# Eight experts on one core: the first two x loads divided by even and odd partitions over two issuing engines

## The chip, the cores and the metric

The kernel runs on 1 core of a Trainium2 chip. The metric is the device time of one execution in microseconds, lower being better; the kernel before has a median of 180.97 us in 3 runs.

## The reference

Eight experts, each with its own 256 tokens, weights and biases, in float32:

```python
# x (8, 256, 512)  w1 (8, 512, 2048)  w2 (8, 2048, 512)  b1 (8, 2048)  b2 (8, 512)
h = np.matmul(x, w1) + b1[:, np.newaxis, :]
h = np.maximum(h, 0)
return (np.matmul(h, w2) + b2[:, np.newaxis, :]).astype(np.float32)
```

## The kernel before

Each expert has two products. The first one, `ph`, is written as 16 groups of 128 hidden columns (`nJ`), each of 4 matmuls over chunks of the 512 inputs (`nKC`). ScalarE reads every group out of PSUM, adds the bias and applies the maximum with zero, which gives `hT` (L231). The second product, `po`, sums 16 of those groups for each of two blocks of 128 tokens. The second product of an expert runs `LAG` = 3 stages behind its first one. A loop of 11 stages on TensorE (`E + LAG`) holds both: matmuls of `ph` are L297, those of `po` L314, the bias b2 as a matmul with ones L324.

Weights come as float32 from HBM and are cast to fp16 by their transfer. All of these transfers are issued by GpSimd at L88 (`load`), 2 MB in SBUF for each of w1 and w2 of an expert, with the loads of x for experts 2 to 7 in two pieces and the stores of experts 0 to 5 behind. They share one queue, q0 in the profile. `NW` = 3 buffers hold w1 and three hold w2. GpSimd waits for a buffer to be free before it issues the load that refills it, so w1 of expert 3 waits for the first product of expert 0. The first weight load waits for the semaphore `s_first`, which a one-row activation on ScalarE (`warm`, L131) raises when it is done.

Ahead of this section, x of experts 0 and 1 is loaded as float32 into `x32[0]` and `x32[1]`, by SyncE, one transfer of 128 partitions with a 4 KB row each (two tokens side by side, `(p tb) h -> p tb h`), in the order expert 0, expert 1. ScalarE issues one transfer for `b1_rows`, 32 rows of 2 KB. Then VectorE casts x of expert 0 to fp16 (L137) and transposes it in 32x32 blocks into `xT` (L124), and ScalarE casts x of expert 1 (L139). All engines but GpSimd enter the section behind these operations, the landing of the x and b1 transfers among them. In the section VectorE turns b1 into `b1T` (L196), which the first activation of `hT` waits for, and then goes on with the transposes of the later experts. SyncE waits for landings and raises a semaphore for TensorE (L246, L247). At the end the stores of experts 6 and 7 leave by SyncE (L251), those two results standing in `x32`.

Of the kernel before, what the change touches and what calls it, by code (L numbers as in the profile page):

```python
# [10 lines left out]
def kernel(  # L11
# [12 lines left out]
    nc = tc.nc  # L24
# [6 lines left out]
    P = 128  # L31
    nTB = T // P
# [15 lines left out]
    def sbuf(name, shape, dtype):  # L48
        return ctx.enter_context(nc.sbuf_tensor(name, shape, dtype))
# [14 lines left out]
    x32 = [sbuf(f"x32_{e}", [P, nTB, H], fp32) for e in range(2)]  # L64
# [42 lines left out]
    def transposes(e):  # L107
# [21 lines left out]

    nc.vector.memset(ones1[:], 1.0)  # L130
    tc.keep_in_program_order(nc.scalar.activation(out=warm[:], in_=ones1[:], func=relu).then_inc(s_first, 1))  # L131
    tc.keep_in_program_order(nc.scalar.dma_start(
        out=b1_rows[:], in_=b1.rearrange("e (b i) -> (e b) i", b=nB)))
    for e in range(2):
        tc.keep_in_program_order(nc.sync.dma_start(
            out=x32[e][:], in_=x[e].rearrange("(p tb) h -> p tb h", tb=nTB)))
    nc.vector.tensor_copy(out=x16[0][0][:], in_=x32[0][:])  # L137
    transposes(0)
    tc.keep_in_program_order(nc.scalar.copy(out=x16[1][0][:], in_=x32[1][:]))  # L139
# [29 lines left out]
    def flush(first):  # L169
        n = GROUPS[first]  # L170
        for tb in range(nTB):
# [7 lines left out]
         in_=b2.rearrange("e h -> (e h)").rearrange("(o f) -> o f", o=1))  # L179
# [15 lines left out]
    for b in range(nB):  # L195
        turned = nc.vector.transpose(  # L196
            out=b1T[b * B : (b + 1) * B, nB - 1 - b : nB - 1 - b + nJ * B],
            in_=b1_rows[:].rearrange("r (i j) -> r j i", j=nJ),
# [23 lines left out]
    for s in range(E + LAG):  # L222
        if s < E:
# [3 lines left out]
            for j in range(nJ):  # L227
# [4 lines left out]
                    out=mine.rearrange("p (tb j k i) -> p j tb k i", tb=nTB, j=nJ, k=split)[:, j],  # L232
                    in_=ph[:, j % NPH, 0:T].rearrange("p (tb i k) -> p tb k i", tb=nTB, k=split),
# [19 lines left out]
    for s in range(E + LAG):  # L253
# [5 lines left out]
        e = s - LAG  # L259
# [112 lines left out]
```

## Time and profile before

| What | Value |
|---|---|
| median of 3 runs | 180.97 us (180.75 to 181.03) |
| profiled execution, its own time | 180.75 us |
| its span in the trace | 179.0 us |
| mean granted TensorE clock | 0.966 |
| busy: PE, DVE, ACT, POOL | 134.6, 86.8, 75.1, 12.7 us |
| HBM read, written | 71.39 MB, 4.19 MB |

The span runs from the first to the last instruction of the program; 1.75 us of the profiled execution's own time lie outside it. DMA shares are of the core's 16 DMA engines together: a share of 1.00 in a stretch of 1 us is 16 us of engine time. Packets are put into the stretch in which they start, so a share in a short stretch can go above 1. q0 is the queue that GpSimd feeds, q1 that of SyncE, q10 that of ScalarE. DMA landings are times from issue until the semaphore of the transfer is complete.

### The profile page before, as it was taken

How to read it: one execution, taken by the hardware profiler on the slowest of the kernel's cores; microseconds unless marked ns; L12 is line 12 of the kernel's file. 1: busy time of each engine (PE TensorE's matmuls, PEld its weight loads, DVE VectorE, ACT ScalarE, POOL GpSimd, SP SyncE). 2: the span in 40 equal slices, each digit the busy share in tenths (PEclk: the TensorE clock that was granted, in tenths of full speed). 3: DMA queues.
4: the chain of work that ended last, by engine and by line, in shares of the span. 5: the costliest groups of instructions: out<-in, count | busy, mean ns of one | idle time of the engine just before them, and what ended most of it. 6: DMA issues, size and time to landing. Idle time of an engine off the chain costs nothing. (4 is left out here: it accounts for less than half of the span.)

```text
span 179.0 us, 3015 instructions
## 1 busy us (share of the span) xinstructions
PE 134.6 (75%) x784; PEld 93.3 (52%) x784; DVE 86.8 (49%) x124; ACT 75.1 (42%) x153; POOL 12.7 (7%) x27
## 2 busy tenths in 40 slices
PE   0004978868699890898988896989698896999960
PEld 0003878858689330785468643884298442434420
DVE  0989938576000299998079916992230003031010
ACT  3201786757677113374087505690387201021010
POOL 4200012020200101001010001000200003010000
PEclk9999999999999999579999999699999999999997
DMA  5989989999999998998999999999899999999996
GB/s 206 277 176 236 234 176 236 231 198 216 236 212 196 236 223 187 234 231 183 231 231 209 205 234 216 194 234 231 179 234 231 194 220 205 222 216 207 330 423 273
DMA packets 3827, 40.46 MB, mean 226 GB/s; under 512 B 449, under 2 KB 465, under 8 KB 1137
## 3 DMA queue, kind: packets, MB, share of 16 engines
q0 software_dynamic: 3200, 38.28, 96.7%
q1 hardware_dynamic: 576, 2.10, 3.0%
q10 hardware_dynamic: 48, 0.07, 0.1%
q14 instruction: 3, 0.02, 0.0%
HBM read 71.39 MB, written 4.19 MB: 422 GB/s over the span
## 5 line engine op out<-in xcount | busy, mean ns | idle before, releaser
L297 PE MATMUL ph<-xT,w_sb 128*128 x512 | 73.2, 307 | 32.5 <-PEq L282 30.1
L297 PEld LDWEIGHTS ph<-xT,w_sb 128*128 x512 | 67.0, 146 | 39.7 <-issue 30.8
L231 ACT ACTIVATE hT<-ph,b1T 128x256 f16<-128x256 f32 x128 | 59.7, 473 | 34.0 <-PE ph L297 30.8
L127 DVE STREAM_TRANSPOSE xT<-x 32x256 f16<-32x256 f16 (+1 forms) x64 | 52.8, 893 | 25.1 <-DMA x<-in_x_dram 21.8
L314 PE MATMUL po<-w_sb,hT 128*128 x256 | 56.6, 379 | 2.2 <-issue 2.2
L314 PEld LDWEIGHTS po<-w_sb,hT 128*128 x256 | 24.9, 97 | 33.0 <-issue 6.9
L211 DVE COPY out<-po 32x512 f32<-32x512 f32 (+1 forms) x20 | 13.8, 688 | 42.8 <-PE po L314 42.6
L211 ACT COPY out<-po 32x512 f32<-32x512 f32 (+1 forms) x20 | 11.5, 577 | 45.9 <-PE po L314 45.7
L88 POOL DMA_DIRECT2D w_sb<-in_w_dram x18 | 9.7, 540 | 137.3 <-PE po L314 70.9
L124 DVE STREAM_TRANSPOSE xT<-x 32x256 f16<-32x256 f16 x32 | 14.0, 436 | 0.5
L211 DVE COPY x<-po 128x512 f32<-128x512 f32 x2 | 1.4, 692 | 13.9 <-PE po L314 13.9
L324 PE MATMUL po<-b_sb,ones 1*128 x16 | 4.8, 378 | 3.7 <-issue 2.3
L211 ACT COPY x<-po 128x512 f32<-128x512 f32 x2 | 1.2, 585 | 14.2 <-PE po L314 14.2
L324 PEld LDWEIGHTS po<-b_sb,ones 1*128 1x128 f16 x16 | 1.5, 91 | 6.5 <-issue 6.2
L196 DVE STREAM_TRANSPOSE b1T<-b_rows 32x512 f32<-32x512 f32 x4 | 4.1, 1025 | 0.5 <-issue 0.5
L139 ACT CAST x<-x 128x1024 f16<-128x1024 f32 x1 | 1.0, 1044 | 3.4 <-DMA x<-in_x_dram 3.4
L137 DVE CAST x<-x 128x1024 f16<-128x1024 f32 x1 | 0.7, 694 | 3.2 <-DMA x<-in_x_dram 3.2
L88 POOL DMA_DIRECT2D out_dram<-out x2 | 1.1, 536 | 9.5 <-DVE out L211 9.5
L131 ACT ACT_TABLE_LOAD x1 | 1.3, 1283 | 0.7 <-PEq L356 0.7
L88 POOL DMA_DIRECT2D x<-in_x_dram x2 | 1.3, 644 | 0.0
L130 DVE MEMSET ones<- 1x128 f16 x1 | 0.2, 165 | 0.9 <-PEq L356 0.9
L88 POOL DMA_DIRECT2D b_sb<-in_b_dram x1 | 0.5, 502 | 0.0
(5 smaller groups left out, 0.7 us busy)
## 6 DMA issues: line engine op xcount, KB each, us to landing
w_sb<-in_w_dram POOLq DMA_DIRECT2D x14, 2048.0 KB, 41.1
w_sb<-in_w_dram POOLq DMA_DIRECT2D x4, 1024.0 KB, 22.3
out_dram<-out POOLq DMA_DIRECT2D x1, 2048.0 KB, 24.7
x<-in_x_dram SPq DMA_DIRECT2D x2, 512.0 KB, 4.0
x<-in_x_dram POOLq DMA_DIRECT2D x1, 1024.0 KB, 34.4
out_dram<-out POOLq DMA_DIRECT2D x1, 1024.0 KB, 17.7
out_dram<-x SPq DMA_DIRECT2D x2, 512.0 KB, 6.8
x<-in_x_dram POOLq DMA_DIRECT2D x1, 512.0 KB, 23.1
```

What stands on the lines that cost most here:

```text
L88: engine.dma_start(**kw).then_inc(landed[key], 16)
L124: last = nc.vector.transpose(out=dst[:, :, g, :, 0, :], in_=block[:, :, :, 0, :])
L127: last = nc.vector.transpose(out=dst[:, tb, g], in_=block[:, tb])
L131: tc.keep_in_program_order(nc.scalar.activation(out=warm[:], in_=ones1[:], func=relu).then_inc(s_first, 1))
L137: nc.vector.tensor_copy(out=x16[0][0][:], in_=x32[0][:])
L139: tc.keep_in_program_order(nc.scalar.copy(out=x16[1][0][:], in_=x32[1][:]))
L196: turned = nc.vector.transpose(out=b1T[b * B : (b + 1) * B, nB - 1 - b : nB - 1 - b + nJ * B], in_=b1_rows[:].rearrange("r (i j) -> r j i" ...
L211: last = copy(out=results[e][at : at + rows, k * nTB + tb, :], in_=po[k * rows : (k + 1) * rows, bank : bank + H])
L231: nc.scalar.activation(out=mine.rearrange("p (tb j k i) -> p j tb k i", tb=nTB, j=nJ, k=split)[:, j], in_=ph[:, j % NPH, 0:T].rearrange("p ...
L297: last = nc.tensor.matmul(ph[:, j % NPH, 0:T], w1_sb[:, bass.ds(w_from + (kc * M + j), P, nJ)], xT[:, bass.ds(x_at + kc * T, T)], start=(k ...
L314: return nc.tensor.matmul(banks[tb], hT[:, bass.ds(h_from + (tb * nJ + j) * P, P)], w2_sb[:, bass.ds(w2_from + j * H, H)], start=False, st ...
L324: nc.tensor.matmul(banks[tb], ones1[:], b2_sb[:, bass.ds(s * H, H)], start=True, stop=False)
```

## The change

Each of the two x loads becomes two transfers of 64 partitions, the even partitions by SyncE and the odd ones by ScalarE, every row still 4 KB. The load of b1 moves from ScalarE to SyncE, behind SyncE's two x halves. The activation that releases the first weight load stands where it stood, ahead of ScalarE's transfers.

```diff
     nc.vector.memset(ones1[:], 1.0)
     tc.keep_in_program_order(nc.scalar.activation(out=warm[:], in_=ones1[:], func=relu).then_inc(s_first, 1))
-    tc.keep_in_program_order(nc.scalar.dma_start(
+    for e in range(2):
+        for odd, engine in enumerate((nc.sync, nc.scalar)):
+            tc.keep_in_program_order(engine.dma_start(
+                out=x32[e][bass.ds(odd, P // 2, 2)],
+                in_=x[e].rearrange("(p tb) h -> p tb h", tb=nTB)[bass.ds(odd, P // 2, 2)]))
+    tc.keep_in_program_order(nc.sync.dma_start(
         out=b1_rows[:], in_=b1.rearrange("e (b i) -> (e b) i", b=nB)))
-    for e in range(2):
-        tc.keep_in_program_order(nc.sync.dma_start(
-            out=x32[e][:], in_=x[e].rearrange("(p tb) h -> p tb h", tb=nTB)))
     nc.vector.tensor_copy(out=x16[0][0][:], in_=x32[0][:])
     transposes(0)
     tc.keep_in_program_order(nc.scalar.copy(out=x16[1][0][:], in_=x32[1][:]))
```

## The prediction

> **What bounds the kernel now.** I read the page first, its DMA row and its queues.
>
> ```profile
> span 179.0 us, 3015 instructions
> DMA  5989989999999998998999999999899999999996
> q0 software_dynamic: 3200, 38.28, 96.7%
> q1 hardware_dynamic: 576, 2.10, 3.0%
> q10 hardware_dynamic: 48, 0.07, 0.1%
> ```
>
> Only the first slice and the last are far from full, and q0, the weights' queue, holds the 16 DMA engines for 96.7% of the span. Next come the windows: the whole stretch with traffic, its two ends, and two pieces of the x loads.
>
> ```profile
> core 0: us, PE busy (x) PEld busy (x) DVE busy (x) ACT busy (x) POOL busy (x), PEclk, DMA share, GB/s
> 1.00:1.50 0.50, 0.00 (x0) 0.00 (x0) 0.08 (x1) 0.50 (x1) 0.00 (x0) 1.00 0.00 0
> 1.50:2.00 0.50, 0.00 (x0) 0.00 (x0) 0.00 (x0) 0.50 (x1) 0.00 (x0) 1.00 0.15 33
> 1.89:3.34 1.45, 0.00 (x0) 0.00 (x0) 0.00 (x0) 0.44 (x2) 0.69 (x2) 1.00 0.93 339
> 3.83:4.90 1.07, 0.00 (x0) 0.00 (x0) 0.61 (x1) 0.00 (x0) 1.07 (x2) 1.00 1.04 371
> 1.89:177.70 175.81, 134.59 (x784) 93.33 (x784) 86.65 (x123) 73.91 (x153) 12.49 (x23) 0.97 1.02 230
> 178.00:179.00 1.00, 0.00 (x0) 0.00 (x0) 0.00 (x0) 0.00 (x0) 0.00 (x0) 0.50 0.00 0
> ```
>
> The engines begin at about 1.89 us and are busy to 177.7 at a mean share of 1.02, TensorE at 134.59 of those 175.81 us. The chain of waits shows how TensorE hangs on this stream and where it ends.
>
> ```profile
> 109.35 39.43 DMA w_sb<-in_w_dram
> 173.09 0.69 DVE x L211
> 165.87 8.34 SPq L251 DMA_DIRECT2D out_dram<-x  x2
> ```
>
> A weight load lands 39.43 us after its issue because loads stand ahead of it in the queue. The last line, from the timeline, gives SyncE's two stores, the second issued right after VectorE's last copy ends at 173.78. Its bytes share the engines with the stores still in q0, and the engines stay full to 177.7. So the end is the start of the traffic, plus the engine time of all bytes, plus holes. The question is whether this change moves any of the three.
>
> **How the start works.** The timeline of the first 17 us, rows picked:
>
> ```profile
> 0.73 1.28 ACT L131 ACT_TABLE_LOAD   x1 [0.73 <-PEq L356]
> 0.74 0.86 SPq L135 DMA_DIRECT2D x<-in_x_dram  x2
> 1.12 0.41 ACTq L132 DMA_DIRECT2D b_rows<-in_b_dram  x1
> 2.03 0.31 ACT L131 ACTIVATE warm<-ones 1x128 f16<-1x128 f16 x1
> 2.65 0.67 POOL L88 DMA_DIRECT2D w_sb<-in_w_dram  x1 [2.20 <-ACT warm L131]
> 4.29 0.69 DVE L137 CAST x<-x 128x1024 f16<-128x1024 f32 x1 [3.21 <-DMA x<-in_x_dram]
> 5.02 7.18 DVE L124 STREAM_TRANSPOSE xT<-x 32x256 f16<-32x256 f16 x16
> 5.69 1.04 ACT L139 CAST x<-x 128x1024 f16<-128x1024 f32 x1 [3.35 <-DMA x<-in_x_dram]
> 12.69 4.14 DVE L196 STREAM_TRANSPOSE b1T<-b_rows 32x512 f32<-32x512 f32 x4 [0.49 <-issue]
> 16.10 9.79 PE L297 MATMUL ph<-xT,w_sb 128*128 x64 [16.10 <-PEq L282]
> 17.25 0.47 ACT L231 ACTIVATE hT<-ph,b1T 128x256 f16<-128x256 f32 x1 [10.51 <-PE ph L297]
> ```
>
> And the queues, from the DMA view of three windows, 3.34:3.83, 0:4.89 and 4.9:6.1 in this order:
>
> ```profile
> q1 hardware_dynamic: 48, 0.13, 67.0%
> q10 hardware_dynamic: 48, 0.07, 36.1%
> ...
> q1 hardware_dynamic: 265, 1.02, 57.0%
> q10 hardware_dynamic: 48, 0.07, 3.6%
> ...
> DMA packets 38, 0.29 MB, mean 242 GB/s; under 512 B 15, under 2 KB 15, under 8 KB 22
> q0 software_dynamic: 16, 0.26, 103.4%
> q1 hardware_dynamic: 22, 0.03, 6.8%
> w_sb<-in_w_dram POOLq DMA_DIRECT2D x1, 2048.0 KB, 32.3
> ```
>
> Up to 4.89 us only q1 and q10 move data; q0's first packets start from 4.9, in the window that holds the last 22 of q1. The weights thus begin when x is done, although their load was issued at 2.65. All 48 packets of b1 lie between 3.34 and 3.83, half-way through x, although b1 was issued at 1.12. The engines were on x until then, so traffic that is ready waits its turn and no engine waits for traffic.
>
> In engine time, x costs 57.0% of 16 x 4.89 us, which is 44.6 us, and 6.8% of 16 x 1.2, which is 1.3: together 45.9, or 2.87 us for each engine. b1 costs 36.1% of 16 x 0.49, which is 2.8 us, or 0.18 an engine. From 1.89 these reach 4.94: the sum agrees with the start of the weights.
>
> **The change part by part.**
>
> *Two halves for each x load.* The same 256 rows of 4 KB go to the same 16 engines, so 2.87 us an engine stay. New are two more transfers to complete, which is two more completion packets on each engine. The last window prices them: its 22 packets of q1 took 1.3 us, of which the 7 that carry the 0.03 MB took about 7 x 0.18 (the 1.04 share of 3.83:4.90 by its 98 packets), and nothing visible is left for the 15 small ones. The bounds are 0 and 0.12 us (a small packet as dear as the mean of q10's 48, 2.8 us / 48 = 0.06); I take 0.02, near the row of q1 itself.
>
> *A hole between the halves.* SyncE's issue of 0.74 shows data at 1.89, 1.15 us later. The odd half of expert 0 is issued at about 1.12, where ScalarE issued b1, and by the same 1.15 us is ready at 2.27. The even half lasts a quarter of 2.87 us, to 2.61. SyncE's half of expert 1, issued at 1.17, is ready at 2.32 too. No hole: 0 us. If ScalarE's queue were later by 0.5 us, SyncE's second half would fill in.
>
> *Earlier first data.* Halving a transfer could shorten the 1.15 us. The issue itself did not scale: 0.43 us each for 128 rows, 0.41 for b1's 32. Bounds: 0 and half the 1.15, or 0.57 earlier; I take 0, near the issue rows.
>
> *b1 moved behind SyncE's two halves.* Third in line, issued at about 1.60, ready at 2.75. Its 0.18 us an engine now come after x's or among them, and the sum does not change with the order. SyncE has nothing to do after it until VectorE's transposes end at 12.20, so its queue pays nothing. If the weights, ready at the earliest at 2.65 + 1.15 = 3.80, slip ahead of b1 or of x1's end, b1 could land after the first weight load, some 10 us late (q0's 16 packets in the window above, one an engine, took 1.24 us each; the load's 128 rows make 8 an engine). Then the section would begin at about 15 instead of 12.2, b1T would end near 20 instead of 16.83, and the first activation would wait 3 us. That has cover:
>
> ```profile
> 26.19 1.05 POOL L88 DMA_DIRECT2D w_sb<-in_w_dram  x2 [20.56 <-PE ph L297]
> 27.47 0.79 PE L297 MATMUL ph<-xT,w_sb 128*128 x4 [1.58 <-PEq L282]
> ```
>
> TensorE idles 1.58 us before expert 1 anyway, waiting for w1. The next weight issue, at 26.19, would slip to 29, while the queue holds the load issued at 5.09 that lands 32.3 us later, at 37.4. The engines do not run dry before that, so the cost is 0; without this cover it would be 3 us.
>
> *x of expert 0 in two landings.* If its odd half alternates with expert 1's even half, it ends up to a quarter of 2.87, 0.72 us, later, and VectorE's chain with it: cast at 5.0, b1T done at 17.5 against an activation at 17.25. TensorE has four banks to write meanwhile, and the 1.58 us: 0.
>
> *The gate.* ScalarE now issues two transfers instead of one, 0.82 us from 1.12, ending at 1.94. The activation is ahead of them in the program and runs at 2.03, behind the table load's end at 2.01. GpSimd's 2.65 stays: 0. If issuing held it up by one issue, 0.41 us, the weights would be ready at 4.2 instead of 3.80 by the estimate, still before x's end at 4.9.
>
> The sum on the profiled execution is 180.75 + 0.02 = 180.77 us (span 179.0 and 1.75 around it). That execution lies 0.22 below the median of 180.97, so on the median's scale I forecast **181.0 us**, no measurable change. About 0.2%, 0.36 us, is what a measurement of this kernel can tell from no change.
>
> **The rivals.**
>
> *Two engines on one door into SBUF: slower.* A half has 4 rows for each engine instead of 8, on every second partition. If four neighbouring rows of a half go to one engine, its partitions spread over eight neighbours, and other engines may write the same part of SBUF at the same moment, each at half rate. At the worst all x rows take twice as long, 2.87 us more an engine, all of it ahead of the weights: 183.8 us. With the engines out of step, about half of it, 1.4 us: 182.4. It decides from 0.36 us, an eighth of the x rows' time. For it: in the row of 1.89:3.34 x with whole transfers runs at a 0.93 share and 339 GB/s, so nothing in x's own pace hides such a loss. Against it: b1 reaches only 32 partitions, and yet 0.07 MB in 2.8 us of engine time is 23 GB/s an engine, as for x (0.40 MB, from 371 GB/s over 1.07 us, in 17.8 us). But b1 is two short rows an engine, which a buffer might swallow.
>
> [...]
>
> *Earlier traffic: faster.* The 1.15 us to first data shrink with the half size, or engines that started last start sooner. Half of it gone gives 180.4; a quarter, 180.7. Against it stand the equal issue times.
>
> *A late start: slower, a little.* The two queues hold each other up or ScalarE's issues delay the gate, and the engines stand idle between x and weights. One issue, 0.41 us, gives 181.4.
>
> *The change does not do what it says* could only mean that ScalarE's transfers come after the cast of expert 1's x. They precede it in the engine's order, so no chance is kept.
>
> **How the numbers follow.** No change by the sum: 0.47. Shared doors: 0.33, nearly all above 0.36 us. Late start: 0.08. Earlier traffic: 0.12. That makes faster 0.12, same 0.47, slower 0.41. The range takes the shared doors up to two thirds of their worst, 2/3 x 2.87 = 1.9 us, which leaves out some 0.1 of chance, and earlier traffic down to 0.4 us: 180.6 to 182.9. The forecast's own range is 180.8 to 181.2.
>
> **What would show it.** Right: q0's first packets start at about 4.9 again, x takes 2.9 us of engine time on q1 and q10 together, the window from 1.89 has a share near 0.93, VectorE's cast starts between 4.2 and 5.0, and the last stores end near 177.7. Wrong: q0 begins at 5.3 or later with packets of x that take longer than before (shared doors) or with a share under 0.9 ahead of it (late start); or the first data come before 1.6 us (earlier traffic). A TensorE that starts later while the end stands still would be right.

## The result

| | before | after |
|---|---|---|
| median of 6 runs | 180.93 us (180.72 to 181.03) | 182.22 us (181.74 to 182.48) |
| ratio | | 1.007, 95% interval 1.0059 to 1.0081 |
| profiled execution, span | 180.75, 179.0 us | 182.02, 180.2 us |

The change costs 1.3 us, 0.7%, with an interval well clear of no change. It is slower, where the forecast was 181.0 us and no change. The time lies outside the forecast's own range of 180.8 to 181.2; the stated range of 180.6 to 182.9 holds it only because it was stretched for the shared doors. The page of the profile after, lines of its first three parts:

```profile
span 180.2 us, 3024 instructions
DMA  5999999999999999999999999999999999999995
q0 software_dynamic: 3200, 38.28, 96.1%
q1 hardware_dynamic: 496, 1.64, 2.4%
q10 hardware_dynamic: 160, 0.52, 1.0%
```

The engines are still full from the second slice to the last but one, and q0 still holds them, so the loss is looked for at the start. Its timeline:

```profile
0.74 1.18 SPq L134 DMA_DIRECT2D x<-in_x_dram  x2
1.12 1.18 ACTq L134 DMA_DIRECT2D x<-in_x_dram  x2
1.96 0.59 SPq L137 DMA_DIRECT2D b_rows<-in_b_dram  x1
2.65 0.67 POOL L88 DMA_DIRECT2D w_sb<-in_w_dram  x1 [2.21 <-ACT warm L131]
4.74 0.69 DVE L139 CAST x<-x 128x1024 f16<-128x1024 f32 x1 [3.66 <-DMA x<-in_x_dram]
6.74 1.04 ACT L141 CAST x<-x 128x1024 f16<-128x1024 f32 x1 [4.40 <-DMA x<-in_x_dram]
17.37 9.90 PE L299 MATMUL ph<-xT,w_sb 128*128 x64 [17.37 <-PEq L284]
```

The gate stands still at 2.65. Each half takes 0.59 us to issue (half of the row of two) where a whole load took 0.43. TensorE's first matmul, which waits for the first weights, moves from 16.10 to 17.37, by 1.27 us. The chain's long wait and VectorE's last copy move by the same amount:

```profile
110.58 39.46 DMA w_sb<-in_w_dram
174.36 0.69 DVE x L213
```

They began at 109.35 and 173.09 before, so the shift is 1.23 and 1.27. The weights land late once, at the start, and nothing later adds to it or takes it back. The windows of the start, after:

```profile
core 0: us, PE busy (x) PEld busy (x) DVE busy (x) ACT busy (x) POOL busy (x), PEclk, DMA share, GB/s
1.50:2.00 0.50, 0.00 (x0) 0.00 (x0) 0.00 (x0) 0.50 (x1) 0.00 (x0) 1.00 0.00 0
2.00:2.50 0.50, 0.00 (x0) 0.00 (x0) 0.00 (x0) 0.33 (x2) 0.00 (x0) 1.00 0.65 238
2.50:3.50 1.00, 0.00 (x0) 0.00 (x0) 0.00 (x0) 0.00 (x0) 0.85 (x2) 1.00 1.08 340
3.50:4.50 1.00, 0.00 (x0) 0.00 (x0) 0.00 (x0) 0.00 (x0) 1.00 (x3) 1.00 0.89 274
```

And the two windows of before that answer to the last two:

```profile
2.50:3.50 1.00, 0.00 (x0) 0.00 (x0) 0.00 (x0) 0.00 (x0) 0.85 (x2) 1.00 0.97 389
3.50:4.50 1.00, 0.00 (x0) 0.00 (x0) 0.21 (x1) 0.00 (x0) 1.00 (x3) 1.00 1.08 381
```

After the change the share drops to 0.89 in the middle of the loads and the rate to 274 GB/s, while x is outstanding: the engines stand partly idle. The hole lies between the halves. The prediction shows the stretch 3.34:3.83 of before, with q1 and q10 at 67.0% and 36.1% of the engines; after the change it has

```profile
q10 hardware_dynamic: 21, 0.06, 52.4%
q1 hardware_dynamic: 5, 0.02, 17.0%
```

ScalarE's first half is running out there, and SyncE's second has hardly begun, although its issue ended at 1.92. The halves of the two engines move in turn. In the change and in the kernel before, the first packet of ScalarE's queue comes just behind the first completion packet (4 bytes, 16 for each transfer) of SyncE's transfer ahead of it (2.742 us behind 2.737 after the change, 3.35 behind 3.34 before). The DMA view of the stretch 0:6.6, first of after, then of before, gives the engine time:

```profile
q10 hardware_dynamic: 160, 0.52, 26.6%
q1 hardware_dynamic: 208, 0.59, 25.5%
q0 software_dynamic: 16, 0.26, 23.6%
```

```profile
q1 hardware_dynamic: 288, 1.05, 43.5%
q0 software_dynamic: 32, 0.52, 37.9%
q10 hardware_dynamic: 48, 0.07, 2.7%
```

x and b1 take 52.1% of 16 x 6.6 us, 55.0 us, against 46.2%, 48.8 us: 0.39 us more packet time for each engine. By 6.6 us 32 weight packets have begun before, two for each of the 16 engines, and 16 after, one for each.

### The profile page after: what moved, and what is told of

The parts are those of the page before. It is cut to its first block, busy times and chain, and to the rows that moved or that the text cites. A ratio compares the mean times of both kernels' runs of the same rounds, so it can differ in the third digit from the quotient of the medians.

```text
span 180.2 us, 3024 instructions
## 1 busy us (share of the span) xinstructions
PE 133.9 (74%) x784; PEld 93.1 (52%) x784; DVE 86.8 (48%) x124; ACT 75.3 (42%) x153; POOL 12.6 (7%) x27
```

## The experiments

Two theories at first. *Shared doors*, a supposition, since the packet records do not tell where an engine writes: in a transfer of 64 partitions several DMA engines write to the same part of SBUF and slow each other. *Two queues*: the loss comes from SyncE and ScalarE feeding the engines at once. The issue of 0.59 us gave a third, *late and slow feeding*: a half reaches the engines later and more slowly than a whole load, and they wait for it. One simple number was taken from every run: how many of the 1.11 MB of x and b1 have begun to move by 4.5 us, before any weight packet. The expectations call the four kernels under "x alone on the engines" e6 to e9, in their order.

**All halves by SyncE**

```diff
-        for odd, engine in enumerate((nc.sync, nc.scalar)):
+        for odd, engine in enumerate((nc.sync, nc.sync)):
 # and b1 by ScalarE, as in the kernel before
```

> Even and odd halves as in the change, but all four by SyncE (even, odd of expert 0, then of expert 1), b1 by ScalarE as before. Shared doors (64-partition transfers make engines collide on SBUF, whichever queue feeds them): x packets again 10 to 20% slower than the 45.6 us of engine time before, engines uneven, 181.6 to 182.2. Two queues (the loss comes from two queues feeding each engine at once): x packets as before, 180.9 to 181.1. Slow issue: if the 0.59 us an issue took is the price of stepping over partitions it stays 0.59 here and the first data come 0.19 later; if it is the price of two engines issuing at once it goes back to 0.43 for SyncE.

Measured: 183.88 us, ratio 1.0162 (1.0149 to 1.0175). One queue is worse than two, so two queues are not needed for the loss. Both expected times were missed.

```profile
0.74 2.45 SPq L136 DMA_DIRECT2D x<-in_x_dram  x4
16.75 1.04 ACT L141 CAST x<-x 128x1024 f16<-128x1024 f32 x1 [14.41 <-DMA x<-in_x_dram]
```

Each issue takes 0.61 us, with only b1 issued by ScalarE beside them, so the price belongs to the half and not to x issued by two engines at once. The fourth half is issued until 3.19, beside the first weights (2.65), and its rows stand among weight packets: expert 1's x is cast at 16.75. No theory had this. The trace records 16 increments for every landing; those of a weight load come 3.1 us apart from first to last, against 0.5 before, and keep that distance to the end.

**Two queues, no division**

```diff
+    for e, engine in enumerate((nc.sync, nc.scalar)):
+        tc.keep_in_program_order(engine.dma_start(
+            out=x32[e][:], in_=x[e].rearrange("(p tb) h -> p tb h", tb=nTB)))
 # b1 behind, by SyncE
```

> Two queues without a division: expert 0's x whole by SyncE, expert 1's x whole by ScalarE, b1 by SyncE behind. Shared doors: as before, 180.9 to 181.1, the first weight packets start together within 0.3 us. Two queues: slow packets and uneven engines as after the change, 181.8 to 182.3. Slow issue: 0.59 with two engines issuing at once, 0.43 if it belongs to stepped partitions.

Measured: 180.89 us, ratio 0.9997 (0.9989 to 1.0006). Two issuing engines cost nothing, and bring nothing.

**The same four transfers and engines, divided by tokens**

```diff
-                out=x32[e][bass.ds(odd, P // 2, 2)],
-                in_=x[e].rearrange("(p tb) h -> p tb h", tb=nTB)[bass.ds(odd, P // 2, 2)]))
+                out=x32[e][:, tb], in_=x[e].rearrange("(p tb) h -> p tb h", tb=nTB)[:, tb]))
```

> The same two engines, order and number of transfers as in the change, each half still all 128 partitions: the first token of each row by SyncE, the second by ScalarE, so 2 KB rows and twice as many packets. Shared doors: no slow packets; twice 512 packets at the 84 ns of b1 rows is 43 us of engine time, about as before, so 180.9 to 181.2. Two queues: as after, 181.8 to 182.4.

Measured: 181.68 us, ratio 1.0049 (1.0037 to 1.0061), a miss for both theories. All 128 partitions are covered and SyncE's two issues take 0.85 us as before, yet 0.49% of the 0.70% is there. (The rows of 2 KB are 512 in all, not twice 512; the 43 us is right for 512.) A division that doubles the rows costs too, whatever the doors.

**Only b1 moved**

```diff
 # x whole by SyncE, as before
-    tc.keep_in_program_order(nc.scalar.dma_start(   # b1, ahead of x
+    tc.keep_in_program_order(nc.sync.dma_start(     # b1, behind x
```

> The kernel before with only b1 moved: third on SyncE behind the two whole x loads. Shared doors and two queues: 180.9 to 181.0, nothing moves. If b1's new place is the loss: 181.5 or more.

Measured: 180.91 us, ratio 1.0001 (0.9992 to 1.001). b1's place is free.

**x alone on the engines.** Four kernels hold the weights back until expert 1's x is cast; all computation stays.

```diff
     tc.keep_in_program_order(nc.scalar.copy(out=x16[1][0][:], in_=x32[1][:]))
+    tc.keep_in_program_order(nc.scalar.activation(out=warm[:], in_=ones1[:], func=relu).then_inc(s_first, 1))
 # and the first activation without its then_inc
# in the fourth: x32[e][lo : lo + P // 2] for lo in (0, P // 2), all by SyncE
```

In this order: the change, the kernel before, even and odd halves by one queue, halves of neighbours by one queue.

> The changed kernel, but the first weight load waits for the cast of expert 1's x (a second one-row activation behind it raises the semaphore), so that x is alone on the engines. Shared doors inside x: x takes about 51 us of engine time or more even alone, with packets of 200 ns and up. Meeting the weights (x packets and weight packets slow each other down, because halves end late and uneven): x takes about 45.6 us again, all packets near 159 ns, and the weight loads start and land within 0.5 us of each other. In both the whole is about 4 us slower than with the early gate, near 185 to 186.

> The kernel before with the same late gate, to compare with e6. Both theories: x at 45 us of engine time, about 185. Shared doors: 0.4 us or more faster than e6. Meeting the weights: within 0.3 us of e6, which then differs by the later first data alone.

> Even and odd halves all by SyncE with the late gate. Shared doors: x at 60 us of engine time or more, since nothing of another queue fills the gaps. Meeting the weights: x at about 45 us, spread over four issues of 0.61 us, so the engines idle between halves and the last half lands near 5.5.

> Halves of 64 neighbouring partitions (0 to 63, then 64 to 127), all by SyncE, late gate. Shared doors: the worst case, a packet near 318 ns and x at 80 to 91 us of engine time if all 16 engines work through half of the doors. Meeting the weights: as e8, about 45 us. Slow issue: 0.43 us an issue if the 0.61 belongs to stepped partitions, 0.61 if to 64 rows.

Measured: the changed kernel 186.35 us (ratio to before 1.0307, 1.0288 to 1.0326), the kernel before 185.34 (1.0244, 1.0227 to 1.0261), and from a single execution each, so without an interval, one queue 186.08 and neighbours 187.67. Between the first two lies a loss of 1.0 us without any weight traffic beside x, so meeting the weights is not the main loss. The DMA view of the stretch 0:8, queue q1 of the kernel before, of one queue, and of neighbours, all with the late gate:

```profile
q1 hardware_dynamic: 288, 1.05, 37.1%
```

```profile
q1 hardware_dynamic: 320, 1.05, 37.8%
```

```profile
q1 hardware_dynamic: 320, 1.05, 55.1%
```

The share times 16 x 8 us is x's engine time: 47.5 us whole, 48.4 by even and odd halves, 70.5 by halves of neighbours. So halves of 64 neighbours make x cost 1.5 times as much, in the direction of shared doors but short of the 80 to 91 us expected of them, and even or odd halves on one queue do not (1.02 times). That the engines slow each other at a shared part of SBUF is not shown by this.

What one queue of even and odd halves shows instead, window 3.50:4.50, the kernel before and then one queue, both with the late gate:

```profile
3.50:4.50 1.00, 0.00 (x0) 0.00 (x0) 0.36 (x1) 0.00 (x0) 0.00 (x0) 1.00 1.07 399
```

```profile
3.50:4.50 1.00, 0.00 (x0) 0.00 (x0) 0.00 (x0) 0.00 (x0) 0.00 (x0) 1.00 0.84 254
```

The packets are as short as before but a sixth of the engines is idle with x outstanding. That is late and slow feeding, alone and without the other two. The whole stretch from the first packet of x and b1 to the end of the last, for the kernel before, the change and one queue, all with the late gate:

```profile
1.75:5.13 3.38, 0.00 (x0) 0.00 (x0) 0.95 (x2) 0.57 (x2) 0.00 (x0) 1.00 0.93 330
```

```profile
2.06:5.96 3.90, 0.00 (x0) 0.00 (x0) 1.06 (x2) 0.28 (x1) 0.00 (x0) 1.00 0.86 286
```

```profile
2.07:6.02 3.95, 0.00 (x0) 0.00 (x0) 0.77 (x2) 0.27 (x1) 0.00 (x0) 1.00 0.81 282
```

The change has its first data 0.31 us later and then needs 0.52 us more, 0.83 of the 1.0 us in all. Of an engine's time 14% of 3.90 us is idle, 0.55 us, against 7% of 3.38, 0.24 us: 0.31 of the 0.52 is idle engines, the rest packet time. For that rest, x and b1 take 20.9% + 20.9% of 16 x 8 us, 53.5 us, against 39.3%, 50.3 us. This part is not the feeding, and it is little more than the spread between kernels: the four with whole loads lie between 47.6 and 50.3 us, in one profile each.

**One transfer on each engine for both experts**

```diff
+    x32_both = sbuf("x32", [P, 2, nTB, H], fp32)
+    x32 = [x32_both[:, e] for e in range(2)]
...
+    for odd, engine in enumerate((nc.sync, nc.scalar)):
+        tc.keep_in_program_order(engine.dma_start(
+            out=x32_both[bass.ds(odd, P // 2, 2)],
+            in_=x[0:2].rearrange("e (p tb) h -> p e tb h", tb=nTB)[bass.ds(odd, P // 2, 2)]))
```

> The same division by even and odd partitions over the same two engines, but one transfer on each for both experts together (64 partitions, two rows of 4 KB each), so two x transfers of 512 KB instead of four of 256 KB, b1 by SyncE behind. Cost of a transfer (a small transfer is ready only 0.7 to 1 us after the one before it, longer than the 0.66 us its bytes take, so engines stand idle and weights get in between): no holes, x near 47 us of engine time, weights start within 0.4 us of each other, 180.8 to 181.2. Cost of the 64-partition shape (issue of 0.6, doors): first data 0.2 to 0.3 late and uneven as after the change, 181.6 or more.

Measured: 181.85 us, ratio 1.0044 (1.0027 to 1.0061). Fewer and larger transfers take off about a third (0.44% against 0.70%) and don't cure it. The number of transfers is thus not the whole price; nor is the 64-partition shape alone, as the division by tokens shows. The DMA view of 0:4.5, then the issues and a window:

```profile
DMA packets 121, 0.50 MB, mean 110 GB/s; under 512 B 0, under 2 KB 0, under 8 KB 121
q1 hardware_dynamic: 121, 0.50, 37.8%
```

```profile
0.74 0.71 SPq L134 DMA_DIRECT2D x<-in_x_dram  x1
1.12 0.70 ACTq L134 DMA_DIRECT2D x<-in_x_dram  x1
3.50:4.50 1.00, 0.00 (x0) 0.00 (x0) 0.00 (x0) 0.00 (x0) 1.00 (x3) 1.00 0.81 233
```

Only 0.50 MB of SyncE's has moved by 4.5 us, at 233 GB/s in the window shown and a share of 0.81. ScalarE's half, issued at 1.12, has not moved a packet. The second half does not fill the holes of the first.

**One expert's x divided**

```diff
+        if e != 0:   # 1 in the second kernel
+            tc.keep_in_program_order(nc.sync.dma_start(
+                out=x32[e][:], in_=x[e].rearrange("(p tb) h -> p tb h", tb=nTB)))
+            continue
```

> Only expert 0's x divided, expert 1's whole by SyncE, b1 behind. Late first data as the main loss: 0.2 to 0.3 us of it here, 181.1 to 181.3. Ragged end of x beside the weights as the main loss: little here, below 181.2, with weight starts within 0.5 us.

> Only expert 1's x divided, expert 0's whole by SyncE ahead of it, b1 behind. Late first data as the main loss: nothing of it here, 180.9. Ragged end beside the weights: most of the loss here, 181.4 to 182.0, weight starts 0.7 to 1 us apart.

Measured: the first alone 181.63 us, ratio 1.0041 (1.0027 to 1.0055); the second alone 181.95, ratio 1.0053 (1.0033 to 1.0072). Either costs more than half, so the parts do not add up to the whole: 0.41% and 0.53% against 0.70%. The first lies above both of its expected times. The second lies where the ragged end was expected to put it, with weight starts even further apart, 5.11 to 6.65 us. In the second kernel the first data come on time, and the holes come with the halves:

```profile
1.50:2.00 0.50, 0.00 (x0) 0.00 (x0) 0.00 (x0) 0.50 (x1) 0.00 (x0) 1.00 0.44 147
2.00:2.50 0.50, 0.00 (x0) 0.00 (x0) 0.00 (x0) 0.33 (x2) 0.00 (x0) 1.00 1.02 393
2.50:3.50 1.00, 0.00 (x0) 0.00 (x0) 0.00 (x0) 0.00 (x0) 0.85 (x2) 1.00 0.79 274
3.50:4.50 1.00, 0.00 (x0) 0.00 (x0) 0.58 (x1) 0.00 (x0) 1.00 (x2) 1.00 0.64 164
```

With the whole load of expert 0 the rate is 393 GB/s; with the halves of expert 1 it falls to 164, at a share of 0.64.

**A later gate**

```diff
+    for _ in range(2):
+        tc.keep_in_program_order(nc.scalar.activation(out=warm[:], in_=ones1[:], func=relu))
+    tc.keep_in_program_order(nc.scalar.activation(out=warm[:], in_=ones1[:], func=relu).then_inc(s_first, 1))
 # behind ScalarE's transfers; the first activation without its then_inc
```

> The changed kernel with three more one-row activations behind ScalarE's transfers, the last of which releases the first weight load, about 1.2 us later. Weights getting in between x's last halves as the cause of the uneven engines: weight starts closer together (under 0.6 us) and no loss against the change in spite of the later gate, 181.9 to 182.3. Late and uneven x by itself: the engines wait longer, 182.6 to 183.2.

Measured: 182.56 us, ratio 1.0087 (1.0062 to 1.0112). It lies between the two expectations and its interval overlaps that of the change, so the time decides nothing. The weights were issued from 3.67 instead of 2.65, and they did not start closer together for it: 5.26 to 6.90 us, in the slowest of the six executions.

The bytes of x and b1 begun by 4.5 us, from the DMA view of 0:4.5 of each:

| kernel | MB by 4.5 us | median us |
|---|---|---|
| two queues, no division | 1.02 | 180.89 |
| only b1 moved | 1.00 | 180.91 |
| before | 0.93 | 180.93 |
| divided by tokens | 0.88 | 181.68 |
| expert 0 divided | 0.77 | 181.63 |
| the change | 0.73 | 182.22 |
| expert 1 divided | 0.71 | 181.95 |
| one queue of halves | 0.70 | 183.88 |
| a later gate | 0.69 | 182.56 |
| one transfer for both | 0.50 | 181.85 |

All kernels with 0.93 or more are at the time of before and all others are slower, but the order among the slower ones is not that of the bytes. Two kernels show why: with one transfer for both, the rest of x then runs at about the rate of the kernel before (369 GB/s in 4.5:5, 426 in 5:5.5, against 381 to 389 there) and the engines begin the weights within 0.6 us of each other; in the one queue of halves the rest waits among the weights, and of the 16 increments of a late weight load (the one complete at 152.56 us) two come 2.4 and 3.0 us behind the first.

## Why the prediction was right or wrong

*What bounds the kernel*: right. The first matmul, the long wait and the last copy moved by 1.23 to 1.27 us with the start of the weights, so time lost ahead of the weights comes out at the end.

*Traffic that is ready waits its turn, and no engine waits for traffic*: carried over wrongly, and read too simply for before. The share of 1.89:3.34 was 0.93, so engines were not all busy there, and b1's first packet came 0.01 us behind the first completion packet of SyncE's first load: it may have waited for that transfer rather than for an engine. It was the basis of the next step.

*A hole between the halves, 0 us*: wrong, and the step that failed. I took the 1.15 us from issue to first data and the 0.43 us of an issue from transfers of 128 partitions, and concluded that the next half would always be there, and that SyncE's second would fill in for a late one of ScalarE. A half takes 0.59 us to issue, after that its rows come more slowly than the engines move them, and the halves move in turn, so none fills in: in 3.50:4.50 the share is 0.89 in the change, 0.84 on one queue with the late gate, 0.64 with expert 1's halves alone. With x alone the idle time of an engine rises from 0.24 to 0.55 us.

*Earlier first data, 0 with bounds of 0 and 0.57 earlier*: the sign was not allowed for. The first data came at 2.08 instead of 1.89, 0.19 us later, close to the extra 0.16 of an issue. The other kernels whose first load is whole have 1.75 or 1.76, so the delay is up to 0.33; but the kernel with only b1 moved gained nothing by its 1.76, so this delay alone need not cost its full length.

*Two halves, 0.02 us for completions at the same 2.87*: too small. x and b1 took 0.39 us more an engine, packets of 4 KB 201 ns in the mean instead of 178. About 3.2 us in 16, 0.2 an engine, are there with two queues and no weights.

*b1 behind, and the gate*: right, by the kernel with only b1 moved and by GpSimd's 2.65. *Late x and late b1 hidden*: the cover was not put to the test on its own; TensorE's start was set by the weights in the change. With one queue, where x landed 11 us late, TensorE did not run first at 16 but at 19.5, and the kernel lost 3 us; in its packet records the load that TensorE waits for before its last three stages ends 3.8 us later on the last engine and 1.8 us later in the mean of the engines, so half of it is the engines left behind.

*Shared doors at 0.33*: longer packets show in halves of neighbours, 1.5 times the engine time, but not in even and odd halves on one queue (48.4 against 47.5 us). No run shows shared doors as their cause, or whether they have a part in the longer packets with two queues. Nor does any show the doubled time of x, or the two thirds of it that the range takes: in the change x and b1 took 1.13 times the engine time (55.0 against 48.8 us). *Late start at 0.08*: the nearest to what happened, engines without work while loads are outstanding, but between halves rather than between x and the weights at the gate, and I priced it at 0.41 us for one issue. The signs named beforehand do not choose between these two: q0 begins at 5.32, with longer packets of x and also with a share under 0.9 ahead of it. That the measured 182.22 lies inside the stated range, and near the 182.4 of the shared doors, is luck, since the sum had only 0.02 us.

The loss can be followed to the first 16 weight packets, counted as one for each engine. In the packet records they end at 7.30 us in the mean and 7.73 for the last, before at 6.28 and 6.46. The mean engine is 1.02 us late, of which 0.19 is later first data, 0.39 longer x and b1, 0.31 longer weight packets (119.6% of 16 x 1.3 us for 16 packets is 1.55 each, where it was 1.24) and 0.13, by subtraction, idle time. The last engine is 1.27 late, because the engines begin the weights further apart (5.32 to 6.31 us, before 4.90 to 5.21). Where x and weights meet, this sum says little on idle against longer packets: records of different queues overlap on an engine, so that in the one queue of halves the packet times up to there make 5.11 us an engine in 4.84 us. The stretch with x alone divides the two better.

Open: the trace does not record what delivers the rows of a 64-partition transfer so slowly, nor why packets are longer with two queues of halves. That tokens on all 128 partitions lose 0.8 us, with first data at 1.75, says that dividing x into more rows costs as well. No version in these runs beats the kernel before: whole loads by two engines are its equal.

## What to carry to other kernels

Where one stream bounds a kernel, ask of every change ahead of it whether the DMA engines stay fed: bytes moved up to a fixed time, and the share while loads are outstanding (in 3.50:4.50, 0.64 to 0.91 in the seven slower kernels of the table, 1.03 to 1.08 in the other three), showed it early here, though the bytes did not order the slower kernels. A load cut in two was not two transfers of half the cost here (0.52 to 0.61 us to issue a half, 0.38 to 0.45 for most whole loads); take its issue time and its first data from a transfer of the same shape, or bound them on both sides. Whole transfers on two issuing engines cost nothing here and gained nothing; cutting a 128-partition load of 512 KB into halves cost time in every form tried, 0.4% to 1.6%.

## What the runs showed of the hardware

- Issues of 128-partition loads took 0.38 to 0.45 us, and 0.56 in the one case behind a half on the same engine; halves of 64 partitions 0.52 to 0.61, 64 partitions with two rows each 0.70 and 0.71. Neighbouring and stepped partitions were alike (2.46 and 2.45 us for four).
- Halves of 64 neighbouring partitions cost 70.5 us of engine time for 1.05 MB, even and odd halves 48.4, whole loads 47.5, in one execution each on one queue.
- With one transfer for both experts, ScalarE's, issued at 1.12 us, had moved no packet by 4.5 us, when 121 of the 128 packets of SyncE's, issued at 0.74, had begun, at a share of 0.81 in 3.50:4.50.
- A distance between DMA engines made early stays: the first and last of the 16 increments of a weight load come 1.0 us apart in the change, 0.5 before and 3.1 with one queue of halves, almost unchanged from about 40 to 165 us. TensorE waits for the last one: in the chain of before its wait ends with it, at 148.78 us.
